# Output projections of a two-layer decoder trunk: weight blocks of 256 channels by 512 columns in place of 512 channels by 256 columns

## The chip, the cores and the metric

The kernel runs on one core of a Trainium2 chip. The metric is the device time of one execution in microseconds (us); of several executions the median is given. TensorE (PE, with its weight loads listed apart as PEld) multiplies, VectorE (DVE), ScalarE (ACT) and GpSimd (POOL) work element by element, SyncE (SP) issues most DMA transfers.

## What is computed

A trunk of two layers over 1024 tokens of width 1024. Layer A is a gated DeltaNet, layer B an attention over a sliding window. Both end in the same kind of step, and that step is what the change touches: the gated head outputs `o`, 1024 tokens by 2048 channels, are multiplied by an output matrix of 2048 by 1024 and added to the residual stream.

```python
def gated_deltanet_mixer(h, w_in, conv_w, a_log, dt_bias, o_gain, w_out):
    ...
    return o.reshape(B, T, A_V_W).astype(h.dtype) @ w_out

def swa_sink_mixer(h, w_in, q_gain, sinks, w_out, k_band, v_band, bias, mask):
    ...
    o = o.reshape(B, T, B_W) * jax.nn.silu(z)
    return o @ w_out

def reference(...):
    x = x + gated_deltanet_mixer(rms_norm(x, a_norm[i]), ...)
    k_band, v_band = shared_kv(x, kv_norm, w_kv, k_gain)
    x = x + swa_sink_mixer(rms_norm(x, b_norm[j]), ...)
```

## The kernel before, in words

Each float32 matrix is held as two parts, `hi` (rounded) and `lo` (what is left), and each product of two matrices is made as three TensorE products: hi by hi, hi by lo, lo by hi. All three accumulate in PSUM.

`out_proj` (L891) makes both output projections. It goes over two halves of 512 tokens; in a half over two column pairs `cp` of 512 output columns; in a pair over four groups `k4` of 512 channels; and in a group over two blocks `b`. For each block it takes one weight block (`take`, L161), and multiplies it for four token blocks `c` of 128 tokens. The stationary operand of a product is a 128 by 128 piece of the head outputs (`oh`, `ol`, held as [128, 4, 512] tiles), the moving operand is a row of the weight block. Before the change a block `b` is 4 times 128 channels by 256 columns, and each token block's PSUM tile `ps[c]` of 512 columns is filled in two separate halves `po`, one for each `b`. With 4 x 3 products for a token block, a weight block gives 48 products of 256 moving columns, and a projection of 32 blocks gives 1536 products, each with its own weight load.

Weight blocks are produced in the order that the generator `weights` (L1334) lists. `weight` (L138) loads 512 KB into `wraw` (two buffers, SP queue, L125), makes `whi` on POOL (L148) and `wlo` on DVE (L152). They are taken one or two blocks ahead. In the second projection the two parts have two buffers each, so that the parts of the block after next can't be made until TensorE has left the block before it.

TensorE's order is the order of the program. The other engines' queues are ordered by the planner of the framework. After each block of two products' rows the kernel calls `tick` (L77), which advances a counter of its own; pieces of work filed with `later` (L73) are put into TensorE's order when the counter reaches their due count. In the first projection that is the turning of the normalized new residual: after the first half of tokens, `finish` files eight groups of four transposes (`turn`, L231 to L243), the first one due 15 ticks later, the others every second tick. A tick stands for six products before the change. When the last block of a column pair is done for a token block, DVE adds the residual (L919) and SP sends the result out (L921). `og_load` (L879) loads the head outputs of the next half, 512 KB at a time, and splits them on ACT (L888) and DVE (L889).

The projection of layer A starts when the last head's work ends and hands over to `kv_part` (L972), which uses the same TensorE engine; the one of layer B is the last stage of the kernel.

Of the kernel before, what the change touches and what calls it, by code (L numbers as in the profile page):

```python
# [7 lines left out]
F32 = mybir.dt.float32  # L8
# [5 lines left out]
ALU = mybir.AluOpType  # L14
# [4 lines left out]
P = 128  # L19
# [45 lines left out]
class Kernel:  # L65
# [825 lines left out]
    def out_proj(self, og, resid, cur, tiles, raws, px, acc, dst, finish):  # L891


        nc = self.nc
        for half in range(2):
            xs, nxt = [], []
            for cp in range(2):
                cs = slice(cp * 512, cp * 512 + 512)
                ps = [acc.tile([P, 2, 256], F32, name="acc") for _ in range(4)]
                for k4 in range(4):  # L900
                    oh, ol = cur[k4]
                    for b in range(2):
                        hi, lo = self.take()
                        if cp == 0 and (k4, b) == (2, 0):
                            self.flush()
                            for c in range(4):
                                xs.append(px.tile([P, D], F32, name="xo", bufs=4))
                                nc.sync.dma_start(xs[c], resid[half * 4 + c])
                        for c in range(4):
                            ts = slice(c * P, c * P + P)  # L910
                            po = ps[c][:, b, :]
                            for kk in range(4):
                                nc.tensor.matmul(po, oh[:, kk, ts], hi[:, kk, :], start=(k4 + kk + b == 0), stop=False)  # L913
                                nc.tensor.matmul(po, oh[:, kk, ts], lo[:, kk, :], start=False, stop=False)  # L914
                                nc.tensor.matmul(po, ol[:, kk, ts], hi[:, kk, :], start=False, stop=(k4 + kk + b == 7))  # L915
                                if kk % 2:
                                    self.tick()
                            if (k4, b) == (3, 1):
                                nc.vector.tensor_tensor(out=xs[c][:, cs], in0=ps[c].rearrange("p b c -> p (b c)"),  # L919
                                                        in1=xs[c][:, cs], op=ALU.add)  # L920
                                nc.sync.dma_start(dst[half * 4 + c][:, cs], xs[c][:, cs])  # L921
                    if half == 0 and cp == 1:
                        nxt.append(tiles(k4))
                        self.og_load(og, 1, k4, nxt[-1], raws)
            cur = nxt
            finish(half, xs)
# [407 lines left out]
    def weights(self):  # L1334

        I = self.I
        rows = lambda name: I[name].rearrange("o (k p) c -> p (o k) c", p=P)
        bin_ = rows("b_w_in")
        col = lambda w, b, gain: (w[:, :, b * P:(b + 1) * P], [KT, P], gain)
        four = lambda w, k, c, gain: (w[:, 4 * k:4 * k + 4, c * 256:c * 256 + 256], [4, 256], gain)  # L1340
        gain = lambda j: self.gcolb[:, 4 * j:4 * j + 4]
        for h in range(AH):
            for b in (8 + h, h, 16 + 2 * h, 17 + 2 * h):
                yield col(self.win, b, None)
            if h == 0:
                yield col(self.win, 32, None)
            if h == 1:
                yield col(self.win, 33, None)
            for i in ([h - 1] if h > 1 and h - 1 not in self.late else []) + ([AH - 1, *self.late] if h == AH - 1 else []):
                for b in (32 + 2 * i, 33 + 2 * i):  # L1350
                    yield col(self.win, b, None)
        for _ in range(2):
            for c in (0, 2):
                for k in range(4):
                    for b in range(2):
                        yield four(rows("a_w_out"), k, c + b, None)
        wkv = I["w_kv"].rearrange("(k p) c -> p k c", p=P)
        for c in range(2):
            for k in range(2):
                yield four(wkv, k, c, gain(k))  # L1360
        for kind, hg, j in self.b_order():
            if kind == "q":
                for k in range(2):
                    yield four(bin_, k, hg, gain(2 + k))
            else:
                yield col(bin_, 16 + 2 * hg + j, self.gcolb[:, 8:16])
        for _ in range(2):
            for c in (0, 2):
                for k in range(4):
                    for b in range(2):  # L1370
                        yield four(rows("b_w_out"), k, c + b, None)

    def dump(self, name, ap):
        self.nc.sync.dma_start(self.dbg[name], ap)
# [21 lines left out]
```

## Time and profile before

| | before |
|---|---|
| median of 3 runs | 1904.08 us (1901.43 to 1906.32) |
| the profiled execution: its own time | 1903.49 us |
| the profiled execution: span, first to last instruction | 1901.7 us |
| PE busy | 1831.0 us (96%), 13186 products |
| PEld busy | 1566.8 us (82%) |
| DVE busy | 1232.2 us (65%) |
| ACT busy | 813.6 us (43%) |
| POOL busy | 517.1 us (27%) |
| mean granted TensorE clock | 0.996 of full speed |
| L913, L914, L915 (both projections) | 1024 products each, of 256 moving columns |

[...] What a product costs in a dense run is the distance from its start to the start of the next one; that distance is read from the timeline. Idle time of an engine that is not the bottleneck costs nothing.

### The profile page before, as it was taken

How to read it: one execution, taken by the hardware profiler on the slowest of the kernel's cores; microseconds unless marked ns; L12 is line 12 of the kernel's file. 1: busy time of each engine (PE TensorE's matmuls, PEld its weight loads, DVE VectorE, ACT ScalarE, POOL GpSimd, SP SyncE). 2: the span in 40 equal slices, each digit the busy share in tenths (PEclk: the TensorE clock that was granted, in tenths of full speed). 3: DMA queues.
4: the chain of work that ended last, by engine and by line, in shares of the span. 5: the costliest groups of instructions: out<-in, count | busy, mean ns of one | idle time of the engine just before them, and what ended most of it. 6: DMA issues, size and time to landing. Idle time of an engine off the chain costs nothing.

```text
span 1901.7 us, 33658 instructions
## 1 busy us (share of the span) xinstructions
PE 1831.0 (96%) x13186; PEld 1566.8 (82%) x13186; DVE 1232.2 (65%) x2868; ACT 813.6 (43%) x1948; POOL 517.1 (27%) x545
## 2 busy tenths in 40 slices
PE   6999999999999998999999999999999999999999
PEld 6677777787878776778999998888788788879999
DVE  6677766768585878765445266787786686753432
ACT  6446353535334353523112043557756656771100
POOL 0332222323232223220211222333433333321111
PEclk9999999999999999999999999999999999999999
DMA  4611111111111111122654321111201111226542
GB/s 148 148 37 39 55 35 56 34 56 45 34 57 34 57 34 57 34 84 95 233 181 153 112 89 45 45 30 51 67 29 51 56 40 51 73 73 196 185 172 80
DMA packets 151267, 149.72 MB, mean 79 GB/s; under 512 B 7242, under 2 KB 124484, under 8 KB 151108
## 3 DMA queue, kind: packets, MB, share of 16 engines
q1 hardware_dynamic: 140768, 130.40, 22.0%
q10 hardware_dynamic: 10340, 17.16, 2.8%
q8 instruction: 104, 1.70, 0.4%
q14 instruction: 55, 0.45, 0.1%
HBM read 116.05 MB, written 31.49 MB: 78 GB/s over the span
## 4 chain that ended last, share of the span: by engine, by line
PE 59%; DVE 20%; issue 8%; ACT 6%; POOL 5%; DMA 1%; SPq 0%; POOLq 0%; ACTq 0%; DVEq 0%
PE mm L177 6%; PE mm L175 6%; PE mm L179 6%; PE acc L914 6%; PE acc L913 6%; PE acc L915 6%; DVE acc L489 4%; PE mm L965 3%; PE mm L967 3%; PE mm L966 3%; DVE wlo L152 2%; ACT lsb L1176 2%; PE pv L1207 1%; POOL acc L486 1%; PE sc L796 1%
## 5 line engine op out<-in xcount | busy, mean ns | idle before, releaser
L175 PE MATMUL mm<-hh,whi 128*128 128x512 f32 (+1 forms) x1040 | 427.2, 411 | 2.3 <-ACT hh L241 2.2
L177 PE MATMUL mm<-hl,whi 128*128 128x512 f32 (+1 forms) x1040 | 417.5, 401 | 1.5 <-DVE hl L242 1.5
L179 PE MATMUL mm<-hh,wlo 128*128 128x512 f32 (+1 forms) x1040 | 415.2, 399 | 0.0
L152 DVE TENSOR_TENSOR wlo<-wraw,whi 128x1024 fp32r<-128x1024 f32 x146 | 184.2, 1262 | 245.7 <-POOL whi L148 219.4
L148 POOL TENSOR_SCALAR whi<-wraw 128x1024 fp32r<-128x1024 f32 x110 | 120.3, 1094 | 504.9 <-PE acc L915 246.4
L175 PEld LDWEIGHTS mm<-hh,whi 128*128 128x128 f32 x1040 | 197.6, 190 | 37.5 <-issue 5.0
L179 PEld LDWEIGHTS mm<-hh,wlo 128*128 128x128 f32 x1040 | 197.2, 190 | 36.2 <-issue 4.2
L177 PEld LDWEIGHTS mm<-hl,whi 128*128 128x128 f32 x1040 | 197.6, 190 | 34.4 <-issue 4.2
L965 PE MATMUL mm<-whi,hh 128*128 128x256 f32 x608 | 180.1, 296 | 0.0
L489 DVE SCALAR_TENSOR_TENSOR acc<-u,cw,acc 128x512 f32<-128x512 f32 x192 | 163.3, 853 | 23.9 <-POOL acc L486 21.8
L967 PE MATMUL mm<-whi,hl 128*128 128x256 f32 x608 | 171.9, 283 | 0.0
L966 PE MATMUL mm<-wlo,hh 128*128 128x256 f32 x608 | 171.8, 283 | 0.0
L913 PE MATMUL acc<-whi,hh 128*128 128x256 f32 x512 | 145.0, 283 | 0.0
L914 PE MATMUL acc<-wlo,hh 128*128 128x256 f32 x512 | 144.9, 283 | 0.0
L915 PE MATMUL acc<-whi,hl 128*128 128x256 f32 x512 | 144.9, 283 | 0.0
L1176 ACT ACTIVATE lsb<-lsb,nm 128x128 f32<-128x128 f32 x256 | 99.8, 392 | 64.2 <-DVE se L1172 54.9
L965 PEld LDWEIGHTS mm<-whi,hh 128*128 128x128 f32 x608 | 115.8, 190 | 11.0 <-issue 10.8
L966 PEld LDWEIGHTS mm<-wlo,hh 128*128 128x128 f32 x608 | 115.9, 191 | 0.2
L967 PEld LDWEIGHTS mm<-whi,hl 128*128 128x128 f32 x608 | 115.6, 190 | 0.0
L486 POOL TENSOR_SCALAR acc<-u,cw 128x512 f32<-128x512 f32 x64 | 63.0, 984 | 181.2 <-ACT u L482 166.8
L1180 POOL TENSOR_TENSOR lsb<-lsb,den 128x512 f32<-128x512 f32 x64 | 68.5, 1070 | 152.6 <-ACT pT L1190 51.5
L914 PE MATMUL acc<-wlo,oh 128*128 128x256 f32 x384 | 108.6, 283 | 0.0
(354 smaller groups left out, 4285.1 us busy)
## 6 DMA issues: line engine op xcount, KB each, us to landing
wraw<-in_a_w_in SPq DMA_DIRECT2D x48, 512.0 KB, 3.9
wraw<-in_a_w_out SPq DMA_DIRECT2D x32, 512.0 KB, 3.7
wraw<-in_b_w_in SPq DMA_DIRECT2D x32, 512.0 KB, 4.0
wraw<-in_b_w_out SPq DMA_DIRECT2D x32, 512.0 KB, 3.7
og<-zs SPq DMA_DIRECT2D x32, 256.0 KB, 2.0
ogT<-zs SPq DMA_DIRECT2D x24, 256.0 KB, 2.1
btab<-lt SPq DMA_DIRECT2D x1, 4096.0 KB, 24.1
dm<-gd SPq DMA_DIRECT2D x8, 512.0 KB, 3.6
```

The source lines that it names most:

```text
L152: nc.vector.tensor_tensor(out=lo, in0=raw, in1=self.f32(hi), op=ALU.subtract)
L175: nc.tensor.matmul(ps, hi[:, k, :], hh[:, k, :], start=(k == 0), stop=False)
L177: nc.tensor.matmul(ps, hi[:, k, :], hl[:, k, :], start=False, stop=False)
L179: nc.tensor.matmul(ps, lo[:, k, :], hh[:, k, :], start=False, stop=(k == KT - 1))
L489: nc.vector.scalar_tensor_tensor(out=acc, in0=u[:, t:t + 512], scalar=cw[:, t, blk:blk + 1], in1=acc, op0=ALU.mult, op1=ALU.add)
L913: nc.tensor.matmul(po, oh[:, kk, ts], hi[:, kk, :], start=(k4 + kk + b == 0), stop=False)
L914: nc.tensor.matmul(po, oh[:, kk, ts], lo[:, kk, :], start=False, stop=False)
L915: nc.tensor.matmul(po, ol[:, kk, ts], hi[:, kk, :], start=False, stop=(k4 + kk + b == 7))
L965: nc.tensor.matmul(ps, hh[:, k, ts], hi[:, k % 4, :], start=(k == 0), stop=False)
L966: nc.tensor.matmul(ps, hh[:, k, ts], lo[:, k % 4, :], start=False, stop=False)
L967: nc.tensor.matmul(ps, hl[:, k, ts], hi[:, k % 4, :], start=False, stop=(k == KT - 1))
L1176: nc.scalar.activation(out=L[:, e, :], in_=L[:, e, :], func=AF.Exp, bias=nm[:, e:e + 1], accum_out=den[:, e:e + 1])
```

## The change

A weight block becomes 256 channels (two rows of 128) by 512 columns. The accumulator of a token block is one PSUM tile [128, 512], which every product covers whole. Two blocks `b` still make up a group `k4`: the first takes rows 0 and 1 of the group's tiles `oh` and `ol`, the second takes rows 2 and 3. `tick` is called after every row, that is after three products instead of after six. The number of weight blocks (32 in each projection), the bytes of a block and the residual add are as before.

```diff
-                ps = [acc.tile([P, 2, 256], F32, name="acc") for _ in range(4)]
+                ps = [acc.tile([P, 512], F32, name="acc") for _ in range(4)]
...
-                            po = ps[c][:, b, :]
-                            for kk in range(4):
-                                nc.tensor.matmul(po, oh[:, kk, ts], hi[:, kk, :], start=(k4 + kk + b == 0), stop=False)
-                                nc.tensor.matmul(po, oh[:, kk, ts], lo[:, kk, :], start=False, stop=False)
-                                nc.tensor.matmul(po, ol[:, kk, ts], hi[:, kk, :], start=False, stop=(k4 + kk + b == 7))
-                                if kk % 2:
-                                    self.tick()
+                            for kk in range(2):
+                                k = 2 * b + kk
+                                nc.tensor.matmul(ps[c], oh[:, k, ts], hi[:, kk, :], start=(k4 + k == 0), stop=False)
+                                nc.tensor.matmul(ps[c], oh[:, k, ts], lo[:, kk, :], start=False, stop=False)
+                                nc.tensor.matmul(ps[c], ol[:, k, ts], hi[:, kk, :], start=False, stop=(k4 + k == 6))
+                                self.tick()
                             if (k4, b) == (3, 1):
-                                nc.vector.tensor_tensor(out=xs[c][:, cs], in0=ps[c].rearrange("p b c -> p (b c)"),
-                                                        in1=xs[c][:, cs], op=ALU.add)
+                                nc.vector.tensor_tensor(out=xs[c][:, cs], in0=ps[c], in1=xs[c][:, cs], op=ALU.add)
...
-            for c in (0, 2):
-                for k in range(4):
-                    for b in range(2):
-                        yield four(rows("a_w_out"), k, c + b, None)
+            for c in (0, 512):
+                for k in range(0, 16, 2):
+                    yield rows("a_w_out")[:, k:k + 2, c:c + 512], [2, 512], None
```

The same edit is made for `b_w_out`.

## Rows read from the trace of the kernel before

**Rows 1.** The page: PE's busy time, and its granted clock in 40 slices.
```profile
PE 1831.0 (96%) x13186; PEld 1566.8 (82%) x13186; DVE 1232.2 (65%) x2868; ACT 813.6 (43%) x1948; POOL 517.1 (27%) x545
PEclk9999999999999999999999999999999999999999
```

**Rows 2.** Busy time by stretch, the two projections: stretch, length, engines, clock, DMA.
```profile
core 0: us, PE busy (x) PEld busy (x) DVE busy (x) ACT busy (x) POOL busy (x), PEclk, DMA share, GB/s
906.00:1095.27 189.27, 188.10 (x1571) 187.89 (x1570) 79.58 (x90) 25.91 (x36) 39.76 (x34) 1.00 0.52 171
1713.30:1897.80 184.50, 184.50 (x1538) 184.36 (x1536) 65.34 (x60) 13.95 (x15) 31.80 (x30) 1.00 0.48 160
```

**Rows 3.** Timeline, PE, second projection: start us, duration us; 1440 products from first to last.
```profile
1719.19 0.28 PE L913 MATMUL acc<-whi,hh 128*128 128x256 f32 x1
...
1891.99 0.28 PE L913 MATMUL acc<-whi,hh 128*128 128x256 f32 x1
```

**Rows 4.** Timeline, PE, first projection: 576 products from first to last.
```profile
930.61 0.28 PE L913 MATMUL acc<-whi,oh 128*128 128x256 f32 x1
...
999.70 0.28 PE L913 MATMUL acc<-whi,kq 128*128 128x256 f32 x1
```

**Rows 5.** Timeline, PE, layer A: a dense run of 512-column products, 45 intervals.
```profile
292.21 0.39 PE L179 MATMUL mm<-hh,wlo 128*128 128x512 f32 x1
...
302.42 0.40 PE L179 MATMUL mm<-hh,wlo 128*128 128x512 f32 x1
```

**Rows 6.** Timeline, PE, layer B: a dense run of 512-column products, 15 intervals.
```profile
1699.60 0.39 PE L175 MATMUL mm<-hh,whi 128*128 128x512 f32 x1
1699.83 0.40 PE L177 MATMUL mm<-hl,whi 128*128 128x512 f32 x1
1700.07 0.39 PE L179 MATMUL mm<-hh,wlo 128*128 128x512 f32 x1
...
1703.10 0.40 PE L175 MATMUL mm<-hh,whi 128*128 128x512 f32 x1
```

**Rows 7.** Timeline, PE, at the second weight block of the first projection.
```profile
911.90 0.28 PE L913 MATMUL acc<-whi,kq 128*128 128x256 f32 x1
913.36 0.39 PE L914 MATMUL acc<-wlo,kq 128*128 128x256 f32 x1 [1.17 <-DVE wlo L152]
```

**Rows 8.** Timeline, DVE, in the same stretch.
```profile
910.96 1.21 DVE L889 TENSOR_TENSOR ol<-dm,oh 128x1024 fp32r<-128x1024 f32 x1
912.09 1.21 DVE L152 TENSOR_TENSOR wlo<-wraw,whi 128x1024 fp32r<-128x1024 f32 x1
```

**Rows 9.** Timeline, PE, first projection: the first group of transposes of the new residual.
```profile
1010.37 0.29 PE L915 MATMUL acc<-whi,vt 128*128 128x256 f32 x1
1010.49 0.60 PE L234 MATMUL tr<-cst,xo 128*128 128x128 f32 x4
```

**Rows 10.** Timeline, DVE: the last residual add of the half, and the scaling.
```profile
999.90 0.69 DVE L919 TENSOR_TENSOR xo<-acc,xo 128x512 f32<-128x512 f32 x1 [0.75 <-PE acc L915]
...
1007.58 2.74 DVE L227 TENSOR_SCALAR xo<-xo,nrs4y 128x1024 f32<-128x1024 f32 x4
```

**Rows 11.** Timeline, all engines, second projection: how a weight block is made.
```profile
1874.96 1.05 POOL L148 TENSOR_SCALAR whi<-wraw 128x1024 fp32r<-128x1024 f32 x1 [4.71 <-PE acc L915]
...
1876.04 1.23 DVE L152 TENSOR_TENSOR wlo<-wraw,whi 128x1024 fp32r<-128x1024 f32 x1 [4.54 <-POOL whi L148]
...
1877.29 0.37 SPq L125 DMA_DIRECT2D wraw<-in_b_w_out  x1
```

**Rows 12.** DMA issues by line: count, KB each, median us from issue to landing.
```profile
wraw<-in_b_w_out SPq DMA_DIRECT2D x32, 512.0 KB, 3.7
...
dm<-ogT ACTq DMA_DIRECT2D x8, 512.0 KB, 5.3
...
oraw<-og ACTq DMA_DIRECT2D x8, 512.0 KB, 5.4
```

**Rows 13.** Line L125, all weight loads: landing time.
```profile
DMA to landing us min/median/max: 3.3/3.9/7.5
```

More of the change, by code (lines that the diff above doesn't have):

```diff
@@ L1367, in weights @@
         for _ in range(2):
[L1368 to L1371, printed above, removed]
+            for c in (0, 512):
+                for k in range(0, 16, 2):
+                    yield rows("b_w_out")[:, k:k + 2, c:c + 512], [2, 512], None
     def dump(self, name, ap):
```

## Prediction

> **What bounds the kernel now.** I read the page first: PE is busy for 96% of the span, at a granted clock of nine tenths or more in each slice [rows 1]. Such an average says little about one stage, so the second view is the busy time by stretch over the two output projections [rows 2]. [...] In both stages what counts is the distance between the starts of products, so the third view is PE's timeline.
>
> In the second projection 1440 products of 256 columns start between 1719.19 and 1891.99 us: 172.80 / 1440 = 120.0 ns each [rows 3]. In the first one, 576 products between 930.61 and 999.70 take 69.09 us, 119.9 ns each [rows 4]. That this is dense and regular, whether DVE, POOL and the DMA queues work or not, says that the pace is TensorE's own.
>
> The price of the new product is in the same trace, since the input projections already use 512 moving columns with the same stationary shape and one weight load each. In a dense run of layer A, 45 intervals between 292.21 and 302.42 us take 10.21 us, 227 ns each [rows 5]. So 512 columns cost 227 ns, where two times 256 columns cost 240 ns. The difference of 227 - 120 = 107 ns for 256 further columns is 2.4 columns a nanosecond; what is left of the 120 ns, some 13 ns, looks like a price of every product whatever its width. The change pays it half as often.
>
> **The products, the one large term.** Before there are 2 x 1536 products: 1536 x 119.9 + 1536 x 120.0 = 368.5 us. After there are 2 x 768 = 1536 products of 512 columns. Priced by the dense run, 1536 x 227 = 348.7 us, so 19.8 us go. All of it is on the path: nothing else ends later than PE in these stages.
>
> The bounds of this price are the two dense runs of 512 columns. In layer B, 15 intervals between 1699.60 and 1703.10 us take 3.50 us, 233.3 ns each; they go up and down (0.23, 0.24, 0.23 us) and do not settle within the run [rows 6]. At that price the saving is 368.5 - 358.3 = 10.2 us. I take 227 ns: the projections are dense for hundreds of products, as the run of 45 is, while the run of layer B is short and lies in a stage where PE changes between kinds of products all the time. Both ends stay for the range.
>
> [...]
>
> **The weight loads into the array.** Half of them go (3072 to 1536). They lie beside the products already, one for each product, and the dense 512-column run contains its own loads, so no term is added.
>
> **The weight blocks.** Their number and bytes stay. Casting a block takes 1.05 us on POOL and 1.23 us on DVE over the same 1024 elements for each partition, and the next load is issued right behind [rows 11]. In the second projection POOL can begin only when PE has left an older block, at 1874.96, and DVE ends at 1877.27. A block now holds PE for 24 x 227 = 5.45 us instead of 5.76, so of a slack of 5.76 - 2.31 = 3.45 us there remain about 3.1. The load itself, with rows of 2 KB instead of 1 KB, is not in this trace as such. Loads of the same 512 KB with 2 KB rows land in 5.3 and 5.4 us, those with 1 KB rows in 3.7 [rows 12]; single ones lie between 3.3 and 7.5 [rows 13]. With two raw buffers a block can come every (landing + 2.3) / 2 us: 2.8 us at 3.3 and 4.9 us at 7.5, below 5.45 at both ends. I take the cost as nothing; PE's own blocks cover it.
>
> **The first stall of the first projection.** PE waits 1.17 us for the second block's `wlo` [rows 7], which DVE makes at 912.09 to 913.30 behind the split of head outputs [rows 8]. None of that is released by PE's products, so the second block starts at the same moment as before, and what the first block saves, 5.76 - 5.45 = 0.31 us, becomes wait. Bounds: the planner may put DVE's queue in another order here, since half the PE instructions around it are gone; the stall could vanish (-1.2) or DVE could do one more operation of 1.2 us first (+1.2). I take +0.3.
>
> **The transposes of the new residual.** They are due 15 ticks into the second half: at 15 x 6 x 0.12 = 10.8 us after its start at 999.70 [rows 4, 9]. The scaling that they need ends at 1007.58 + 2.74 = 1010.32 on DVE, a chain that starts from the last residual add at 999.90 [rows 10]; so the margin is 0.17 us. A tick is now three products of 227 ns, and 15 of them are 10.2 us, 0.57 us earlier. The chain does not get faster. PE therefore waits about 0.57 - 0.17 = 0.4 us at the first group. Behind PE's wait only products stand in the queue, and no buffer runs out in 0.4 us. Bounds 0 to 0.6. The seven other groups come every two ticks, 1.4 us, and find the scaled rows ready.
>
> **With one answer.** The residual add still reads 512 columns of one bank, after the same last product of a token block. The second block of a group needs rows 2 and 3 of the head outputs only, later than before, and nothing waits for them now. The end of the kernel behind the last product (add, store) is unchanged.
>
> **The sum.** -19.8 + 0.3 + 0.4 = -19.1 us. The profiled execution took 1903.49 us, which gives 1884.4. The median of the runs is 0.59 us above that execution, so I expect a median of 1885.0 us, 1.0% less.
>
> **The rivals.**
> - *The pace does not settle.* One or both projections keep the up-and-down pace of layer B's run, 233.3 ns [rows 6]: 768 x 6.3 ns = 4.8 us more for each, 1889.8 with one and 1894.6 with both. For it: it is the nearest run in time to the second projection, with the same tiles as moving operand. Against it: 45 intervals of rows 5, and that the same projections keep an even 120.0 now.
> - *The planner reorders a queue.* DVE or ACT near the start or between the halves serves another piece first, and PE waits at a few places; at 1.2 us a place (one DVE cast) and four places, 1890.
> - *The pace goes with the columns.* 512 columns cost 2 x 120 = 240 ns, the price of every product being hidden in something else here: no gain, and the two small waits remain, 1904.8. The single 0.24 us intervals of rows 6 are for it, both means are against it. [...]
> - *Slower: the weight loads become the bound.* If 2 KB rows made the loads slow, PE would wait for each of the 64 blocks. With two buffers it decides from a landing of 2 x 5.76 - 2.3 = 9.2 us on, where a block again takes 5.76; at 10 us a block takes 6.15, which is 64 x 0.39 = 25 us more than now, 1929. Against it: 5.3 and 5.4 us for such rows, and 7.5 as the longest of all weight loads.
>
> That the change might not do what it says, with a 512-column product made as two, is excluded by rows 5: there it is one instruction with 227 ns.
>
> **How the numbers follow.** Chances: forecast 0.62; unsettled in one projection 0.16, in both 0.08; reordering 0.06; pace with the columns 0.05; loads 0.03. About 0.3% (5.7 us) is what a measurement of this kernel can tell from no change. Faster by more, below 1898.4: 0.62 + 0.16 + 0.08 + 0.06 = 0.92; within it 0.05; slower 0.03. The low end: the first stall and the wait at the transposes vanish, 1885.0 - 1.2 - 0.3 - 0.4 = 1883.1, and the median moves by about a microsecond from set to set: 1882. The high end takes in one unsettled projection and the reordering, 1890 and 1.5 for the same spread: 1891.5. Outside lie 0.16.
>
> **What would show it.** Products of L913 to L915 after the change: 512 of each line, starting 227 ns apart; projections of about 189.3 - 9.2 = 180.1 and 184.5 - 9.9 = 174.6 us; the wait for `wlo` at the second block about 1.5 us; a wait of PE for DVE at the first group of L234 in the first projection; no waits for weights elsewhere. Distances of 233 ns would show the first rival, 240 the third, waits of PE on weights in each block the last. A changed length outside these two stretches would show that I missed a part.

## The result, and the profile after

The changed kernel takes 1891.62 us (median of four, 1890.04 to 1893.31), the kernel before 1904.62 us in the same comparison: a ratio of 0.9934, 95% interval 0.9917 to 0.9951. It is faster by 13.0 us where 19.1 were forecast. The profiled execution took 1890.78 us, its span is 1889.1 us.

First the page of after: busy time by engine, TensorE's granted clock, the queue named `q8 instruction`; beside it the same row of the kernel before, which was not shown yet.

```profile
PE 1814.9 (96%) x11650; PEld 1484.9 (79%) x11650; DVE 1231.8 (65%) x2868; ACT 812.8 (43%) x1948; POOL 512.9 (27%) x545
PEclk9999999999999999999999999999999999999999
q8 instruction: 92, 1.51, 0.3%
```
```profile
q8 instruction: 104, 1.70, 0.4%
```

The 1536 products that went are there (13186 to 11650, [rows 1]), and so is the clock. Queue 8 moved 12 packets less. That row gets its meaning further down.

Busy time by stretch, the two projections after (columns as in [rows 2]):

```profile
907.23:1090.36 183.13, 181.91 (x804) 147.33 (x802) 83.01 (x90) 24.81 (x33) 38.24 (x34) 1.00 0.51 175
1710.87:1885.30 174.43, 174.39 (x770) 144.06 (x768) 63.49 (x61) 14.36 (x15) 32.22 (x30) 1.00 0.49 168
```

The second is 10.1 us shorter than in [rows 2], the first only 6.1. Cutting both profiled executions at the first product of the first projection, at the first one behind it, and at the first one of the second projection gives the whole account:

| stretch, us | before | after | change | forecast |
|---|---|---|---|---|
| ahead of the first projection | 906.06 | 907.23 | +1.2 | 0 |
| first projection | 189.21 | 183.13 | -6.1 | -9.2 |
| between the projections | 618.07 | 620.51 | +2.4 | 0 |
| second projection and end | 188.37 | 178.19 | -10.2 | -9.9 |

So 3.1 us are missing in the first projection, 2.4 us were lost between the projections, where nothing was edited, and 1.2 us ahead of everything. The last is no work of the change: the kernels below that share this part of the program need 902.7 to 909.4 us for it in their profiled executions, and the kernel before, profiled once more, 906.81.

How the pace looks now, from PE's timeline (start us, duration us). Second projection, 720 products from first to last:

```profile
1716.46 0.39 PE L913 MATMUL acc<-whi,hh 128*128 128x512 f32 x1
...
1879.66 0.39 PE L913 MATMUL acc<-whi,hh 128*128 128x512 f32 x1
```

163.20 us / 720 = 226.7 ns from one start to the next, beside a recorded duration of 0.39 us: the price that was taken from [rows 5]. First projection, the starts of three blocks in a row, 24 products apart:

```profile
925.51 0.39 PE L913 MATMUL acc<-whi,oh 128*128 128x512 f32 x1
...
931.11 0.40 PE L913 MATMUL acc<-whi,oh 128*128 128x512 f32 x1
...
936.59 0.40 PE L913 MATMUL acc<-whi,oh 128*128 128x512 f32 x1
```

5.60 / 24 = 233.3 ns in one block, 5.48 / 24 = 228.3 in the next, and over the projection the lengths repeat: 5.61, 5.60, 5.48 us. The weight blocks go round three places: two buffers of the pool `wsp` and one of the pool `wx`. The short ones, 11 of 32, are those in `wx`. The others keep the up-and-down pace of [rows 6] to their end.

Behind the first projection PE waits for the first norm, at L234; in brackets stand the idle time and what ended it. The timeline of PE after, and behind it that of before:

```profile
1099.29 0.55 PE L234 MATMUL tr<-cst,xo 128*128 128x128 f32 x3 [1.14 <-DVE xo L227]
```
```profile
1103.06 0.55 PE L234 MATMUL tr<-cst,xo 128*128 128x128 f32 x3 [0.32 <-DVE xo L227]
```

1.14 us where it was 0.32. The timelines of DVE and POOL just ahead of that, again after and then before:

```profile
1086.21 2.10 DVE L152 TENSOR_TENSOR wlo<-wraw,whi 128x1024 fp32r<-128x1024 f32 x1 [4.38 <-ACT whi L151]
1085.34 1.90 POOL L150 TENSOR_TENSOR wraw<-wraw,gcolb 128x1024 f32<-128x1024 f32 x1 [1.75 <-DMA wraw<-in_w_kv]
```
```profile
1090.85 1.23 DVE L152 TENSOR_TENSOR wlo<-wraw,whi 128x1024 fp32r<-128x1024 f32 x1 [4.53 <-ACT whi L151]
1091.74 2.09 POOL L150 TENSOR_TENSOR wraw<-wraw,gcolb 128x1024 f32<-128x1024 f32 x1 [3.67 <-DMA wraw<-in_w_kv]
```

After, DVE's last weight cast comes upon a multiplication that POOL has begun, and takes 2.10 us instead of 1.23; before, POOL came later. The last residual adds follow that cast on DVE; behind them come the squares on ACT and the norm on DVE, for which PE waits. These first 25 us behind the projection are called the handover below.

### The profile page after: what moved, and what is told of

Its sections match the earlier page's. It is cut to its first block, busy times and chain, and to the rows that moved or that the text cites. A ratio compares the mean times of both kernels' runs of the same rounds, so it can differ in the third digit from the quotient of the medians.

```text
span 1889.1 us, 30600 instructions
## 1 busy us (share of the span) xinstructions
PE 1814.9 (96%) x11650; PEld 1484.9 (79%) x11650; DVE 1231.8 (65%) x2868; ACT 812.8 (43%) x1948; POOL 512.9 (27%) x545
## 4 chain that ended last, share of the span: by engine, by line
PE 60%; DVE 20%; issue 8%; ACT 5%; POOL 5%; DMA 2%; POOLq 0%; SPq 0%; DVEq 0%; ACTq 0%
PE mm L177 7%; PE mm L175 7%; PE mm L179 7%; PE acc L915 6%; PE acc L914 6%; PE acc L913 6%; DVE acc L489 4%; PE mm L963 3%; PE mm L965 2%; PE mm L964 2%; DVE wlo L152 2%; PE pv L1205 2%; ACT lsb L1174 1%; POOL acc L486 1%; PE sc L796 1%
## 5 line engine op out<-in xcount | busy, mean ns | idle before, releaser
L913 PE MATMUL acc<-whi,hh 128*128 128x512 f32 x256 | 99.7, 390 | 0.0
L915 PE MATMUL acc<-whi,hl 128*128 128x512 f32 x256 | 99.6, 389 | 0.0
L914 PE MATMUL acc<-wlo,hh 128*128 128x512 f32 x256 | 99.6, 389 | 0.0
L150 POOL TENSOR_TENSOR wraw<-wraw,gcolb 128x1024 f32<-128x1024 f32 x36 | 72.9, 2026 | 94.4 <-DMA wraw<-in_b_w_in 65.8
```

The costliest lines, as they stand in the source:

```text
L913: nc.tensor.matmul(ps[c], oh[:, k, ts], hi[:, kk, :], start=(k4 + k == 0), stop=False)
L914: nc.tensor.matmul(ps[c], oh[:, k, ts], lo[:, kk, :], start=False, stop=False)
L915: nc.tensor.matmul(ps[c], ol[:, k, ts], hi[:, kk, :], start=False, stop=(k4 + k == 6))
```

## Experiments

Two questions: what sets the pace of the products in the first projection, and what happens between the projections. Times are against the kernel before in the same comparison, 1904.4 to 1905.4 us.

### What sets the pace: the places of the operands

The candidates were the density of the run (the argument of the prediction), the halves of a partition's memory (operands on the same side settle, those on two sides don't), and the byte offset of the two operands, alike modulo 64 or modulo 256. By the program's memory map, modulo 256: `wsp` lies at 64, `wx` and all head outputs of the first projection at 224, the moving tiles of layer B and the head outputs of the second projection at 64, layer B's own weight buffers at 192.

**Products alone, all places.** Only a run of rows like this one, over copies of one input tile:

```python
for j in range(n):
    nc.tensor.matmul(bank, big[:, s + (j % 3) * P:][:, :P], big[:, m_j:m_j + 512], start=(j == 0), stop=(j == n - 1))
```

> This kernel measures the pace alone: it leaves the whole trunk out and runs products of 512 moving columns from one tile of 196 KB for each partition, 24 in a row for each pair of places of the stationary and the moving operand (13 places), then with the stationary operand shifted by 4 bytes to 2 KB, then four runs of 240. Theory 1 (halves): a row settles at 227 ns where both operands lie below, or both above, a boundary between byte 110400 and byte 122848 of the partition, and stays at 231 to 234 ns where they lie on different sides; the shifts change nothing. Theory 2 (alignment): all pairs of the grid, multiples of 4096 bytes apart, settle at 227 ns, and a shift by 32 bytes, not by 64, gives 233 ns. Theory 3 (history): the pace depends on what went before a row, not on places; no order by place is seen.

Measured: 226.7 ns for every pair of places that are multiples of 4 KB apart, on one side or on two (but for the very first row, whose first dozen products stand 427 ns apart). With the stationary operand shifted by 4, 8, 16, 32, 64 and 128 bytes: 232.3, 230.8, 233.3, 233.3, 233.3 and 231.7 ns; by 256, 512, 1024 and 2048 bytes: 226.7. The same at three pairs of places, and a row of 240 products stays where it settled. The halves fall, and 64 bytes is not the modulus. 256 is what is left (theory 4 from here on).

**All weights of the first projection in `wsp`, or all in `wx`.**

```diff
-                    self.wpools, self.wcount, self.depth = [self.wsp, wx, self.wsp], 1, 2
+                    self.wpools, self.wcount, self.depth = [self.wsp], 0, 1
```

> The changed kernel with all weight blocks of the first projection in the two low buffers (bytes 28480 to 44864), none in the third one at byte 131040. Theory 1 (halves) and theory 2 (alignment modulo 64 bytes): the blocks of 5.48 us disappear, all take about 5.61 us, and the first projection takes 183.1 + 10 x 0.13 = 184.5 us, 1.3 us more than the changed kernel. Theory 3 (history at the start of a row): with two buffers, as in the second projection, the blocks settle at 5.44 us and the projection takes about 177 to 180 us.

Measured 1896.01 us, ratio 0.9952 (0.9938 to 0.9967). Every block without other work in it takes 5.60 us. One takes 9.92: with two buffers PE waits 2.72 us for `wlo` there, and from 924.96 to 928.37 us, from that wait on, the granted clock is 0.50. The projection takes 187.14 us, 2.6 more than expected.

```diff
-                    wx = pool(c2, "wx", side="right")
-                    self.wpools, self.wcount, self.depth = [self.wsp, wx, self.wsp], 1, 2
+                    wx = pool(c2, "wx", 2, side="right")
+                    self.wpools, self.wcount, self.depth = [self.wsp] + [wx] * 31 + [self.wsp] * 2, 1, 1
```

(`vv` was moved behind `wx` to make room.)

> The changed kernel with all blocks of the first projection but the first in two high buffers (bytes 122848 to 139232), for which the place of vv is given free until later. Theories 1 and 2: all blocks take 5.44 to 5.48 us, the first projection 183.1 - 20 x 0.13 = 180.5 us, and the kernel about 2.6 us less than the changed one, 1889. Theory 3: no difference of place, blocks of 5.6 us remain, 183 us or more.

Measured 1893.77 us, 0.9942 (0.9927 to 0.9957). Every block but the first two and those with the transposes takes 5.44 us, the projection 179.75 us, 0.3 less than the forecast of the prediction. The time is not lower for it: the stretch between the projections grew to 627.18 us, 6.7 more than in the changed kernel, at the handover: PE is idle for 3.42 us there, and behind that the granted clock is 0.50 for 6.8 us. So it is the buffer's place, not the projection, its tiles or its density. These two runs don't tell sides from offsets; the next two do.

**The same buffers, moved by 32 or 160 bytes.** An unused tile ahead of `wsp`:

```diff
+            ctx.enter_context(tc.tile_pool(name="pad", bufs=1)).tile([P, 8], F32, name="pad")
```

> The changed kernel with a pad of 32 bytes ahead of the weight buffers, so that the low buffers begin at a multiple of 64 plus 32, as the head outputs do; all stay in their half. Theory 1 (halves): as in the changed kernel, two of three blocks of the first projection take 5.61 us and one 5.48, 183.1 us. Theory 2 (alignment modulo 64): all blocks take 5.44 to 5.48 us, 180.5 us. Theory 3: no statement on places, as in the changed kernel.

Measured 1890.51 us, 0.9926 (0.991 to 0.9943): blocks of 5.59, 5.60 and 5.45 us, the projection 182.67. At offset 96, which is like 224 modulo 64, `wsp` is still slow. With `[P, 40]` it lies at 224:

> The changed kernel with a pad of 160 bytes ahead of the low weight buffers: their first byte goes from 64 to 224 modulo 256, which is what the head outputs of the first projection (byte 155616 and on) and the third weight buffer (131040) have; the second projection's operands move together and stay alike. Theory 4 (both operands alike modulo 256 bytes): all 32 blocks of the first projection take 5.44 to 5.48 us, none 5.61, and it takes 183.1 - 21 x 0.13 = 180.4 us; the second one stays at 174.4; the kernel takes about 2.7 us less than the changed one. Theory 1 (halves of the partition): no buffer changes its half, so two of three blocks keep 5.6 us, 183.1 us. Theory 2 (alike modulo 64) gives the same as theory 4 here.

Measured **1887.21 us** (1886.46 to 1891.7), 0.9921 (0.9909 to 0.9933). All blocks without other work in them take 5.44 us. PE's timeline, the start of a block in `wsp` and that of the next one, 24 products later:

```profile
926.17 0.39 PE L913 MATMUL acc<-whi,oh 128*128 128x512 f32 x1
...
931.61 0.39 PE L913 MATMUL acc<-whi,oh 128*128 128x512 f32 x1
```

And the projection, with PE's busy time:

```profile
908.09:1087.97 179.88, 178.48 (x803) 147.33 (x802) 83.03 (x90) 24.60 (x32) 38.03 (x34) 1.00 0.53 177
```

5.44 / 24 = 226.7 ns. 179.88 us is 3.25 less than after, from a tile of 160 bytes that nothing uses. The forecast had 180.1. The whole times alone would not tell this kernel from the changed one, since the intervals of the two ratios overlap; the projection's length does, with 182.67 to 183.13 us in the changed kernel, with 32 bytes and in the kernel below that is wide in the first projection alone, and 179.88 to 180.06 in every version with 160 bytes.

**Products alone, what the offset is relative to.** As the first run, with both operands shifted alike, one of them alone, and other widths.

> The whole block is left out; only rows of fp32r products with a new stationary tile of 128 columns each stand in it, 48 products per row, over copies of one input tile, and shifts are in elements of 4 bytes. Theory 4 (what counts is how far the two operands lie apart, modulo 256 bytes): stationary and moving shifted alike by 8, 16, 32, 40 or 48 elements repeat every 226.7 ns in every row; the moving operand alone shifted by 8 to 48 elements gives 230 to 234 ns on average, by 64 elements 226.7; the stationary alone gives 226.7 at 64, 128 and 192 elements only, and 230 to 234 at 24, 40, 48, 56, 60, 63, 65 and 96. The 480 products at 32 elements stay at about 232 to their end. With 256 columns every row has a mean of 120.0 ns whatever the shift. Rival (the place of the stationary operand by itself decides): rows shifted alike by other than 0 are at 230 to 234, and rows with the moving operand alone shifted at 226.7. Rival (a long row settles whatever the places): the 480 products at 32 elements reach 226.7.

Busy time by stretch, one row of products each (length, PE busy and count, clock, DMA):

```profile
76.38:87.07 10.69, 10.69 (x48) 1.00 0.00 0
131.30:142.22 10.92, 10.92 (x49) 1.00 0.00 0
231.31:241.96 10.65, 10.65 (x48) 1.00 0.01 2
253.08:264.00 10.92, 10.92 (x48) 1.00 0.00 0
501.75:613.06 111.31, 111.31 (x480) 1.00 0.03 10
```

Each stretch runs from the first start to the last, so it holds 47 intervals, in the last row 479. The first row is both operands shifted by 128 bytes, 10.69 / 47 = 227.4 ns with its first products, 226.7 once settled; the second the moving operand alone by 128 bytes, 232.3. So the distance between the operands counts, not the place of one: the moving operand shifted by 160 or 64 bytes gives the 234.3 and 228.8 ns that the stationary one gives when shifted by 96 or 192. The third and fourth are the stationary operand shifted by 252 and by 260 bytes: 226.6 and 232.3. The last is 128 bytes over 480 products: 232.4 to the end. In the kernel the slow blocks lie 224 - 64 = 160 bytes apart, with the pad of 32 bytes 128; rows at these shifts have 233.4 and 232.4 ns here, 24 times of which is 5.60 and 5.58 us, within some 0.02 us of those blocks.

Three expectations were missed. Shifts of 240 and 252 bytes settle too, so the good place reaches a little below the multiple of 256. At 192 bytes the pace is 228.8, below the range named. And with 256 columns the offset does not leave 120.0 alone: at shifts of 32, 64 and 128 bytes the mean is 118.3, 117.8 and 118.6 ns, faster than in place, where 512 columns are slower. With 384 columns it is 173.3 in place and 176.1 at 128 bytes.

**Layer B's weights in place as well.** 128 bytes more, ahead of layer B's weight buffers:

```diff
+                    pool(c2, "padb").tile([P, 32], F32, name="padb")
```

> The last but one version (160 bytes ahead of layer A's weight buffers) with 128 bytes more ahead of layer B's weight buffers, so that these lie at 224 modulo 256 bytes like that layer's moving tiles. Theory 4: the first projection stays at 179.9 us and the products of layer B's input weights repeat every 227 ns instead of 231 to 233, which is worth some us only where TensorE is never waiting there; layer B waits for other engines between its products, so at most 1 us comes off the time, 1886 to 1888 us. Rival (layer B is bound by TensorE's products): 12 column blocks with about 100 products each at 5 ns less give up to 5 us, 1882 us. Rival (the moved buffers alter nothing): as the version without the second pad.

Measured 1890.55 us, 0.9922 (0.9908 to 0.9936), the same ratio as without it; a gain from the moved buffers can't be told from this. But the longest runs of layer B, of 15 intervals as in [rows 6], settle now. The end of one of them, PE's timeline:

```profile
1694.78 0.39 PE L175 MATMUL mm<-hh,whi 128*128 128x512 f32 x1
1695.01 0.39 PE L177 MATMUL mm<-hl,whi 128*128 128x512 f32 x1
...
1696.37 0.39 PE L177 MATMUL mm<-hl,whi 128*128 128x512 f32 x1
```

From the second row to the third are six products: 1.36 / 6 = 227 ns. This is the same short run in the same stage, so density did not decide in [rows 6]. Over all unbroken runs of that kind in layer B the mean fell only from 233.4 ns in the kernel before to 232.2, since these runs took seven to ten products to settle (the one above 1.39 us, 232 ns each, for its first six intervals, 1693.39 to 1694.78), and 132 of the 135 runs have five intervals or fewer.

### Where the 2.4 us between the projections come from

**One projection wide, the other narrow.** `out_proj` and the weight list as before for one of the two:

> Only the first projection has blocks of 256 channels by 512 columns, the second one is as before. If the loss against the forecast sits in and right behind the first projection: the projection takes 183.1 us (189.2 before), the stretch between the projections is 0.8 to 1.5 us longer than before because of the wait for the scaled residual behind it, the second projection takes 184.5, so 4.5 to 5.5 us less than before, 1899.5. If the layer between the projections loses for another reason (its own queues), its stretch is 2.4 us or more longer.

> Only the second projection has blocks of 256 channels by 512 columns. All theories of the pace: 174.4 us for it (184.5 before), nothing else moves, so 10.1 us less than before, 1894.5. If the stretch between the projections is longer here too, its loss does not come from the first projection.

Measured: first alone 1900.17 us, 0.9977 (0.9968 to 0.9986), with a projection of 183.07 and 621.05 us between. Second alone 1894.94 us, 0.9958 (0.9945 to 0.997), with 178.19 us for it and the end. Between the projections it has 620.59 us, but not of the same make: nothing at the handover and nothing in the first 300 us of layer B, and 2.1 us at some 400 to 450 us, where PE was idle for 3.81 us and the granted clock was then 0.50 for 6.8 us (before: 2.67 us idle, then 3.4 us). The kernel before, profiled once more, shows how much of such sums is the run:

> The kernel before once more, unchanged, for a second profile of the stretches that the change does not touch: if the start (906.06 us to the first projection) and the stretch between the projections (618.07 us) move by 1 to 3 us from run to run by themselves, the 1.2 and 2.4 us that the changed kernel has more there are no effect of the change; if they come out within some 0.3 us, they are.

Measured 1904.44 us, with 618.35 between, 0.3 more than the first profile, and 0.0 at the handover. So the handover of +1.1 belongs to the wide first projection.

The 2.4 us are a sum of more lost and something given back. Compared product by product, from the first one behind the projection on, the changed kernel is 1.1 us behind the kernel before at 20 us, 2.8 at 300 and 4.2 at 420, but 2.7 at 440. In between both wait for POOL, and the same 17 products follow. PE's timeline at that wait, first before, then after:

```profile
1517.16 0.96 PE L1186 MATMUL tp<-cst,lsb 128*128 128x128 f32 x4 [2.67 <-POOL lsb L1180]
```
```profile
1516.42 0.66 PE L1184 MATMUL tp<-cst,lsb 128*128 128x128 f32 x4 [3.14 <-POOL lsb L1178]
```

And the stretch of the 17 products (length, PE busy and count, clock, DMA), before and after:

```profile
1517.16:1520.79 3.63, 3.63 (x17) 0.53 0.19 72
```
```profile
1516.42:1518.53 2.11, 2.11 (x17) 1.00 0.00 0
```

Before, the granted clock is 0.50 from 1517.38 to 1520.79 us, behind an idle of 2.67 us. After, it stays at 1.00, behind a longer one. That gives back 1.5 us; without it layer B loses 2.8 us and not 1.3. Why the clock stayed up is not shown.

**POOL's multiplication out of the way.** The version with 160 bytes, without the gain on the second block of the key and value weights:

```diff
-                yield four(wkv, k, c, gain(k))
+                yield four(wkv, k, c, None if c else gain(k))
```

> Leaves out the multiplication by the norm's gain on the second column block of the key and value weights (GpSimd, line 150), in the version with 160 bytes ahead of layer A's weight buffers. If the handover behind the first projection is late because VectorE's last weight cast runs beside that multiplication, the cast takes 1.23 us in place of about 2.1 and TensorE's wait for the first norm behind the projection falls by 0.9 to 1.1 us, from about 1.4 to 0.4 us. If it is late because the weights land late, the wait stays above 1 us. If the 1.3 us that layer B loses are a result of the late start, the whole stretch between the projections falls by over 2 us, from 620.9 to below 619; if not, to 619.7 to 620.

DVE's last cast, and PE at the first norm behind the projection:

```profile
1084.80 1.23 DVE L152 TENSOR_TENSOR wlo<-wraw,whi 128x1024 fp32r<-128x1024 f32 x1 [4.21 <-ACT whi L151]
1096.10 0.90 PE L234 MATMUL tr<-cst,xo 128*128 128x128 f32 x4
```

The cast is back at 1.23 us, the wait is gone, and 25 us behind the projection the kernel is 1.65 us ahead of the version with 160 bytes: the handover is settled. The time is 1888.49 us, of a single run. Between the projections it has 619.68 us, which is about the range named for the case that layer B's loss is no result of the late start. This sum by itself is blurred, since here the granted clock was 0.50 from 1513.48 to 1516.89 us, where the version with 160 bytes kept 1.00. The kernel before had such a stretch too, and against it layer B takes 1.9 us more, though the handover is 0.3 us shorter: the late start is not the cause.

**The weight loads of layer B.** With every wide first projection two loads of 512 KB in layer B, issued some 122 and 212 us behind it, take longer. The second one in the timeline, SP's issue and POOL's multiplication that waits for it, first before, then after:

```profile
1307.58 0.37 SPq L125 DMA_DIRECT2D wraw<-in_b_w_in  x1
1311.33 1.90 POOL L150 TENSOR_TENSOR wraw<-wraw,gcolb 128x1024 f32<-128x1024 f32 x1 [5.20 <-DMA wraw<-in_b_w_in]
```
```profile
1304.12 0.37 SPq L125 DMA_DIRECT2D wraw<-in_b_w_in  x1
1309.00 1.90 POOL L150 TENSOR_TENSOR wraw<-wraw,gcolb 128x1024 f32<-128x1024 f32 x1 [6.33 <-DMA wraw<-in_b_w_in]
```

3.75 us from issue to multiplication before, 4.88 after. First suspicion: rows of 2 KB in place of 1 KB in the projection's loads. Two DMAs of 256 columns for each wide block, again on the version with 160 bytes:

```diff
-        self.nc.sync.dma_start(raw, src)
+        for c in ((slice(0, 256), slice(256, 512)) if shape == [2, 512] else (slice(None),)):
+            self.nc.sync.dma_start(raw[:, :, c], src[:, :, c])
```

> The version with 160 bytes ahead of layer A's weight buffers, with each wide weight block of 256 channels by 512 columns loaded by two DMAs of 256 columns (rows of 1 KB, as in the kernel before) in place of one with rows of 2 KB. In every version with the wide first projection the load of layer B's input weights that is issued some 212 us behind that projection has its GpSimd multiplication 4.6 to 5.4 us after the issue, in those with the narrow one 3.7 to 3.95. Theory A (the rows of the projection's loads set how the later loads fall): it comes 3.7 to 4.0 us after the issue again, the last key and value load lands as in the kernel before, and the stretch between the projections falls from 620.9 us by 1 to 2.8 us, the time by 1 to 2 us. Theory B (it has to do with something else that the wide first projection shifts): 4.6 to 5.4 us again, and a stretch of 620.5 to 621.5. In both the products of both projections repeat every 227 ns, and the projections take 179.9 and 174.4 us; a first stall up to 0.5 us longer, because the second half of a load is issued 0.4 us later.

Measured **1886.78 us** (1885.54 to 1889.49), 0.991 (0.9893 to 0.9927). The multiplication comes 4.9 us behind the issue again, the load at 122 us takes 5.16: the rows of the loads are not it. Between the projections it has 619.52 us, 1.3 less than the version with 160 bytes and outside what was expected for this case; why, this run does not tell.

The packets of queue 8 are the second suspect. They are 16 KB each (1.70 MB / 104), and 12 of them went with 1536 products and their 1536 weight loads, 3072 instructions: one for each 256. In the first projection they come some 15 us apart before, 27 to 30 after. Where they fall against a load, from the trace's packet records (us behind the load's issue):

| kernel | load at 122 us: packet, landing | load at 212 us: packet, multiplication |
|---|---|---|
| before | 2.67, 3.52 | 2.84, 3.74 |
| second wide alone | 3.29, 3.88 | 3.23, 3.95 |
| after | 2.20, 4.97 | 2.18, 4.88 |
| 160 bytes | 1.10, 4.86 | 1.11, 5.29 |

To move these packets and nothing else, products of zeros at the very start, 92 of them (184 instructions) or 128 (256 instructions, a whole packet):

```python
for _ in range(2):
    ps = self.mm.tile([P, 512], F32, name="mm")
    for i in range(n):   # n = 46 or 64
        nc.tensor.matmul(ps[0:16, 0:64], z[:, 0:16], z[:, 16:80], start=(i == 0), stop=(i == n - 1))
```

> The version with 160 bytes ahead of layer A's weight buffers, with 92 products of 16 by 64 zeros on TensorE at the very start, 184 instructions that compute nothing that is used. Theory (instruction fetches): the 12 packets of 16 KB fewer on queue 8 are TensorE's instructions, one packet for each 256 of them, 128 products; a packet that starts while a weight load of 512 KB is under way makes that load land 1.0 to 1.8 us later. 184 instructions more put every packet 72 instructions later in the program than one packet earlier: in the first projection from 16.2 us ahead of its end to 8.1 us ahead, where the second key and value load, issued 8.3 us ahead, lands after about 5 us in place of 3.4; GpSimd's multiplication then starts 3.2 us ahead of the end in place of 4.75, VectorE's last cast takes 1.23 us in place of 2.3, and TensorE's wait behind the projection falls by about 1.1 us. In layer B the packets fall some 4.3 us later: the load 122 us behind the projection lands after 3.5 to 4.0 us, the one at 212 us has its multiplication 3.7 to 4.0 us behind its issue. The stretch between the projections falls from 620.9 to 618 to 619.7 us (other loads may be hit). Rival (the late landings have nothing to do with the packets): 3.4 us for the key and value load, 2.3 us for the cast, 4.6 to 5.4 us at the load at 212 us, and a stretch of 619.5 to 621.5. The zeros cost 0 to 5 us ahead of everything.

> The same with 128 products of zeros, 256 instructions. Theory (instruction fetches, one packet for each 256): one packet more, and every later packet at the same place of the program as without the zeros: key and value load 3.4 us, VectorE's last cast about 2.3 us, the load at 122 us 4.8 to 5.1 us and the multiplication at 212 us 4.6 to 5.4 us behind its issue, the stretch between the projections 620.3 to 621.5 us. Rival (it is the zeros themselves, or that everything starts later, that alters the stretch): as with 92 products. The zeros cost 0 to 7 us ahead of everything.

Measured: 1887.28 us, 0.991 (0.9885 to 0.9936), and 1888.19 us, 0.9915 (0.989 to 0.9941), like the version with 160 bytes: the zeros run from 1.06 us to 5.91 and to 7.27 us, and in the kernel before TensorE waits until 6.50 us for its first data. The packets went where the count said: with 184 instructions the one at 16.2 us ahead of the projection's end stands at 8.1, with 256 all stand where they were. SP and POOL in the timeline at the load at 212 us, first with 184 instructions of zeros, then with 256:

```profile
1300.79 0.37 SPq L125 DMA_DIRECT2D wraw<-in_b_w_in  x1
1304.74 1.89 POOL L150 TENSOR_TENSOR wraw<-wraw,gcolb 128x1024 f32<-128x1024 f32 x1 [5.41 <-DMA wraw<-in_b_w_in]
```
```profile
1301.05 0.37 SPq L125 DMA_DIRECT2D wraw<-in_b_w_in  x1
1306.27 1.90 POOL L150 TENSOR_TENSOR wraw<-wraw,gcolb 128x1024 f32<-128x1024 f32 x1 [6.68 <-DVE pT L1192]
```

3.95 us against 5.22; the load at 122 us 3.85 against 5.07. So the packets of TensorE's instructions delay these two loads, by 1.27 and 1.22 us here, and that explains the late landings. At the handover the theory failed: with the packet 0.2 us behind its issue the key and value load landed after 3.49 us as without one, the cast took 2.41 us and the wait stayed. Between the projections: 620.66 and 621.31 us, 0.65 apart. The granted clock fell at the same places in both, so these two compare, and 620.66 lies outside the 618 to 619.7 that the theory gave. The load at 122 us has no part in it: in all these kernels POOL's multiplication comes 6.6 us behind its issue, whether it lands early or late.

## Point by point

**What bounds the kernel**: right. In the second projection PE is busy for 174.39 of 174.43 us, in the first but for 183.13 - 181.91 = 1.22 us, both at a granted clock of 1.00 as before [rows 2].

**The products, -19.8 us**: the step that failed, in its size: it came to about 16.5 us. The second projection went by 227 ns and gave 10.1 us where 9.9 were forecast. In the first one 21 of 32 blocks kept 233.3 ns: 21 x 24 x 6.6 ns = 3.3 us less than forecast. The prediction had both prices [rows 5, 6], named the unsettled pace as a rival, and chose between them by the density of the run. Density is not what tells them apart: with other offsets the same 15 intervals of [rows 6] settle, and 480 dense products at a bad offset don't. The rival as it stood, one whole projection unsettled for 4.8 us, was two thirds right. What was missing was to ask in what the two runs differ, and they differ in which buffers feed them. The names of the tiles are in the rows; the memory map of the program has the offsets. The even 120.0 ns of the projections now [rows 3, 4] was taken as evidence for settling and was none: at the offsets of the first projection 256 columns give 120.0 as well.

**The price of every product, some 13 ns**: right with the operands in place. In the runs of products alone such products repeat every 120.0, 173.3 and 226.7 ns at 256, 384 and 512 columns: 53.3 ns for each 128, with 13.3 ns left over.

**The weight loads into the array, the weight blocks**: right, both at nothing. PE waits for weights nowhere but at the first stall. The blocks with rows of 2 KB land in 3.6 us (median), like those with rows of 1 KB before (3.7 [rows 12]), not in the 5.3 that the prediction took as a bound.

**The first stall, +0.3**: right in kind, smaller here. PE's timeline after:

```profile
914.53 0.50 PE L914 MATMUL acc<-wlo,kq 128*128 128x512 f32 x1 [1.22 <-DVE wlo L152]
```

The product that waits for the second block's `wlo` starts 7.30 us behind the projection's first product, before (913.36 - 906.06 [rows 7]) as after (914.53 - 907.23), so what the first block saves does become wait. At the slow pace it saved 0.16 us (5.68 us instead of 5.84). The recorded idle time grew by 0.05 only (1.22 against 1.17), because the product ahead of the wait is recorded 0.11 us longer.

**The transposes, +0.4**: no wait in the changed kernel. PE after, at the first group, and DVE's last scaling:

```profile
1008.28 0.60 PE L234 MATMUL tr<-cst,xo 128*128 128x128 f32 x4
```
```profile
1005.69 2.74 DVE L227 TENSOR_SCALAR xo<-xo,nrs4y 128x1024 f32<-128x1024 f32 x4
```

They come 10.39 us into the half (997.89) instead of the 10.2 that the settled pace would give. The scaling ends at 1008.43, 0.15 us behind the start of the group, but its last row is needed only by the group's last transpose. The row's own end was taken as the moment that the first transpose needs. With 160 bytes the group does come at 10.2 us, and there a wait shows inside it, at the last transpose: the group takes 0.88 us instead of 0.60.

```profile
1007.10 0.88 PE L234 MATMUL tr<-cst,xo 128*128 128x128 f32 x4
```

**Between the projections, 0**: missed, +2.4, which is 3.9 lost and 1.5 given back where the granted clock stayed up. About 1.1 us is the handover. A shorter last block starts DVE's cast 0.28 us nearer to the end, and the cast meets POOL's multiplication, because the load behind it landed after 3.34 us instead of 5.26. The collision is shown, by the run without the multiplication. That the load landed sooner because a packet of queue 8 no longer fell on it (before: 1.07 us behind its issue) is argued: the run meant to put one there had it 0.2 us behind the issue, and nothing happened. The other 2.8 us are in layer B. The late landings there are shown to come from the instruction packets (5.22 us against 3.95 with the packets moved); but putting them right brought 0.65 us. In the kernels with a wide first projection layer B takes 1.1 to 2.8 us more than before where the granted clock falls at some 420 us as it did before, and 0.1 to 1.4 more where it stays up. What else makes up these sums stays open.

**The sum.** 1884.4 us was forecast for the profiled execution, it took 1890.78: +3.1 in the first projection, -0.3 in the second, +2.4 between, +1.2 ahead, together 6.4. That the miss is not larger is luck in part: 1.5 us of the losses between the projections were given back where the granted clock stayed up. The range ended at 1891.5, with one unsettled projection but nothing for the rest of the kernel. The larger lost part, 3.25 us of the first projection, can be had back with 160 unused bytes: such kernels took 1887.2 us, or 1886.8 with split loads, which the measurements don't tell apart.

## To carry to other kernels

Before a price is taken from another place of the trace, ask which buffers feed that place: two runs of the same product at 227 and 233 ns differed in nothing but the byte offset between their operands, and a few unused bytes ahead of a pool moved all products of the first projection to the better one. A stage that gets shorter shifts the phase of everything behind it, so a load that was late can be early, and the work behind it collide with that of another engine (here a load landed after 3.34 us in place of 5.26, and a cast took 2.10 us in place of 1.23); put a microsecond or two for that into the range, also where nothing is edited. When such losses are added up, compare the granted clock of the stretches too: here 1.5 us of it stood against 3.9. Look at the queue of instruction packets when a load takes a microsecond longer for no reason in its own queue: here 5.22 us against 3.95.

## What the runs showed of the hardware

- In the runs of products alone the pace of products of 512 columns with a new stationary tile each depended on the distance between the stationary and the moving operand modulo 256 bytes: 226.7 ns at 0 and at 240 and 252, 228.8 to 234.3 at 4 to 224. At 256 columns it was 120.0 in place and 117.8 to 120.1 elsewhere. Why is open; the DMA share of the rows shown above was 0.00 to 0.03.
- Two VectorE operations on two tiles that met a GpSimd multiplication ended only behind it: a cast of 1.23 us took 2.10 and ended at 1088.31, 1.07 us behind GpSimd's end at 1087.24; without the multiplication it is back at 1.23. In the kernel before, an operation on 128x4 elements, 0.16 us elsewhere, took 1.68 us until GpSimd's operation of 1311.33 ended at 1313.23:

```profile
1311.56 1.68 DVE L1178 TENSOR_TENSOR den<-den,se 128x4 f32<-128x4 f32 x1 [1.56 <-ACT lsb L1176]
```

- In these kernels TensorE's instructions came in packets of 16 KB (1.70 MB / 104), one for each 256 instructions: 12 packets went with 3072 instructions, and 184 instructions of zeros moved the packets by the time of 72. Loads of 512 KB with a packet that started 1.0 to 2.6 us behind their issue landed 0.5 to 1.9 us later than the same loads without one, those with one 0.0 to 0.3 us or 2.7 to 3.3 us behind did not. One load does not fit: the one 321 us behind the projection took 5.3 to 5.6 us in six of the kernels, with a packet 2.8 to 3.4 us behind its issue (5.36 with one at 2.9 in the version with 160 bytes). That packets delay loads is shown by the two runs with zeros, at the loads at 122 and 212 us (3.85 against 5.07 us, 3.95 against 5.22); the times behind the issue are read off all the kernels, and no run set them one by one.
